# Left-side sums one group earlier, and down's first seven products one plain step earlier, in parts two and three of a macaron FFN

## The chip, the cores and the metric

The kernel runs on one core of a Trainium2 chip. The metric is the device time of one execution in microseconds; of several runs the median is taken. Before the change it is 1948.83 us (3 runs, 1947.93 to 1949.49).

## What is computed

One decoder block on a sequence of 256 tokens with 2048 channels, in float32: half an FFN, a mixer of two kinds of attention, half an FFN again, a gated embedding, a last norm. The change lies in the two FFNs:

```
D_MODEL, SEQ, D_FF = 2048, 256, 5632

def swiglu(x, w_gu, w_down):
    gate, up = jnp.split(x @ w_gu, 2, axis=-1)
    return (jax.nn.silu(gate) * up) @ w_down

h = h + 0.5 * swiglu(rms_norm(h, ffn1_norm[i]), ffn1_w_gu[i], ffn1_w_down[i])
h = h + hybrid_mixer(...)
h = h + 0.5 * swiglu(rms_norm(h, ffn2_norm[i]), ffn2_w_gu[i], ffn2_w_down[i])
gate = jax.nn.sigmoid(rms_norm(h, ple_norm[i]) @ ple_w_gate[i])
h = h + gate * (p[i] @ ple_w_proj[i])
return rms_norm(h, final_norm)
```

## The kernel before

**Split products.** Every float32 weight tile of 256 rows by 512 columns (raw, 128 x 1024 on chip) is split in two: ScalarE rounds it to its high half (whi, line 77), VectorE subtracts for the low half (wlo, line 78). The left sides are split likewise (nTh and nTl from the norm, hTh and hTl from the hidden activations). A product is then three matmuls: high times high, high times low, low times high. One such weight tile makes a *plain step*: 12 matmuls (lines 543 to 545), for two halves of 128 rows and two halves of 128 tokens.

**Seven products.** Part of each matrix product is done by a scheme with seven block products in place of eight (Strassen's, in Winograd's form). It needs sums of weight blocks and sums of left-side blocks. The weight blocks lie in four tiles R0 to R3; lines 307 and 314 add them up (on VectorE, or by an accumulating DMA on POOL's queue), line 298 (ScalarE, shi) and line 299 (VectorE, slo) split a sum; two buffers each. The left-side sums are made in `halves`: S = high + low (line 455), four subtractions and additions (line 461), and the split into Sh (ScalarE, line 463) and Sl (VectorE, line 464). `product` (lines 342 to 344) issues one of the seven, 3 matmuls for each of `ns` blocks of 128 rows (k rows of the contraction in pairs; ns is 4 for gate/up, 3 for down in parts two and three), and copies or subtracts what it has in its bank (lines 347, 350 and 352). Products 0, 4 and 6 read the left sides themselves, the others Sh and Sl.

**Parts and groups.** The hidden width is worked through in three parts of 3, 4 and 4 blocks of 512 (`PARTS`). A part has a *group* "gu" for each block (gate and up, 512 columns each, four PSUM banks), then two groups "dn" (two blocks of 512 output columns each). A gu group of parts two and three has 8 plain steps. While a group goes through its plain steps, the seven products of the *following* group are issued between them. `plan` writes this order by hand: `at[j]` is the plain step behind which the j-th product comes (in the order `SEVEN`), and `order` lists the weight splits in the same order; `next_weights` issues them some steps ahead, one sum ahead at most. `first` is the plain step of the first product: 1 between groups of one kind, 2 between kinds, 8 and 4 in two special cases. With 2, the last two products fall on one plain step, as the list is cut off at the group's last step.

**The work beside the products** runs in lanes: generators which go one step on behind each plain step (`lanes.step`). `halves` is one of them, in lane 1. `down_input` is another, in lane 0: it makes hTh and hTl of a finished gu group (line 480 on VectorE for sil, 485 for the transposition, DMAs through DRAM from ScalarE's queue and SP's, lines 502 and 503 for the split); it takes a whole group and is finished by force at the end of the next. Within this, a scheduler sets the final order of each engine's instructions; each engine works through its own in order.

The left-side sums of the first dn group of a part read the first hidden blocks of the part. Before the change `halves("dn", ...)` is added at the start of the last gu group of the part; it makes two blocks at once in its first step (1024 columns, four 256-wide steps on S), and the third in a later step (512 columns, 128-wide steps).

Of the kernel before, what the change touches and what calls it, by code (L numbers as in the profile page):

```python
# [46 lines left out]
def block_kernel(ctx, tc, a, out):  # L47
# [306 lines left out]
    def plan(n):  # L354


        def sources(name, blk):

            q, pairs = a[name + "q"][blk], a[name][blk]
            return [q[:, :, g, :].rearrange("j p n -> p j n") for g in range(q.shape[2])] + \  # L360
                [pairs[g] for g in range(pairs.shape[0])], q

        groups = []
        for p, (i0, i1) in enumerate(PARTS):
            for i in range(i0, i1):
                plain = PLAIN[n]
                if i < plain:
                    src = [([a[f"w_gu{n}0"][2 * i + b][g] for g in range(KD // 2)], None) for b in range(2)]
                else:
                    src = [sources("w_gu" + n, 2 * (i - plain) + b) for b in range(2)]  # L370
                groups.append(Group("gu", p, [x[0] for x in src], [x[1] for x in src], NS if i >= plain else 0,
                                    len(groups) % 2))
            for nb in (0, 2):
                src = [sources(f"w_down{n}{p}", nb + b) for b in range(2)]
                groups.append(Group("dn", p, [x[0] for x in src], [x[1] for x in src], NS_DOWN[p], len(groups) % 2, nb))
        if n == "2":
            src = [sources("w_behind", b) for b in range(2)]
            groups.append(Group("behind", len(PARTS), [x[0] for x in src], [x[1] for x in src], NS_BEHIND,
                                len(groups) % 2))
        if n == "1":  # L380

            groups[0].plain.sort(key=lambda x: x[1])
        made, carried = [], []
        for i, group in enumerate(groups):
            group.follower = follower = groups[i + 1] if i + 1 < len(groups) else None
            after = groups[i + 2] if i + 2 < len(groups) else None
            n_plain = len(group.plain)
            at, loads, carried = [], {0: carried}, []
            if follower is not None and follower.ns:
                first = 8 if not group.ns else 4 if follower.kind == "behind" else \  # L390
                    1 if group.kind == follower.kind else 2
                at = [min(first + j, n_plain - 1) for j in range(7)]
                if not group.ns:
                    follower.first = n

                    loads.setdefault(max(at[0] - 5, 0), []).extend(follower.loads())
                if after is not None and after.ns:
                    *three, last = after.loads(follower)
                    for x, one in zip((4, 5, 6), three):
                        loads.setdefault(at[x], []).append(one)  # L400
                    carried = [last]
            todo = []
            for j, (b, g) in enumerate(group.plain):
                todo.append(("plain", (b, g)))
                order.append(("pair", group.src[b][g]))
                if group.kind == "behind" and g == KD // 2 - 1:
                    order.append(("pair", a["w_pp"][b]))
                for x in range(7):
                    if at and at[x] == j:
                        todo.append(("seventh", x))  # L410
                        order.append(("sum", follower))
                order.extend(loads.get(j, []))
            made.append((group, todo))
        return made
# [5 lines left out]
    order += [("pair", a["w_pg"][2][g]) for g in range(KD // 2)] + [("pair", a["w_pp"][2])]  # L420
    order.append(("pair", a["w_pp"][3]))

    def halves(kind, his, los, ns, wait=0):


        for _ in range(wait):
            yield
        fp = current[0]

        sh = fp.tile([P, NS, 2, 2, P], F32R, tag="Sh", name="Sh")  # L430
        sl = fp.tile([P, NS, 2, 2, P], F32R, tag="Sl", name="Sl")

        def side(i, g):
            if i in (0, 4, 6):
                k, t = 2 * (g % 2) + (i > 0), i // 6
                c = slice(t * P, (t + 1) * P)
                return his[g // 2][:, k, c], los[g // 2][:, k, c]
            j, t = {1: (1, 1), 2: (0, 0), 3: (0, 1), 5: (1, 0)}[i]
            return sh[:, g, j, t, :], sl[:, g, j, t, :]

        sides[kind] = side

        for g0 in range(0, ns, 2):
            n = min(2, ns - g0)
            hi, lo = his[g0 // 2], los[g0 // 2]
            keep = lambda ins: ins
            if g0 and n == 1:

                keep = tc.keep_in_program_order
                yield  # L450
            if n == 2:
                x = fp.tile([P, 2 * NB], F32, tag="sil", name="S")
            else:
                x = act.tile([P, NB], F32, tag="nat", name="S", bufs=4)
            keep(nc.vector.tensor_tensor(out=x, in0=hi[:, 0:2 * n].bitcast(F32).rearrange("p k x -> p (k x)"),
                                         in1=lo[:, 0:2 * n].bitcast(F32).rearrange("p k x -> p (k x)"), op=ALU.add))
            xv = x.rearrange("p (g j t y) -> p g j t y", g=n, j=2, t=2)
            a11, a12, a21, a22 = (xv[:, :, j, t, :] for t in range(2) for j in range(2))
            for o, y, z, op in ((a22, a21, a22, ALU.subtract), (a21, a11, a21, ALU.subtract),
                                (a11, a22, a11, ALU.subtract), (a12, a11, a12, ALU.add)):  # L460
                nc.vector.tensor_tensor(out=o, in0=y, in1=z, op=op)
            sx = [y[:, g0:g0 + n].rearrange("p g j t y -> p (g j t y)") for y in (sh, sl)]
            nc.scalar.copy(sx[0], x)
            nc.vector.tensor_tensor(out=sx[1], in0=x, in1=sx[0], op=ALU.subtract)
            yield

    def ffn(n, nT, r, scale, next_norm, stat):
        xs = picker(*nT)
        late = callable(r)
        with tc.tile_pool(name="ffn", bufs=1) as fp:  # L470
# [43 lines left out]
            for group, todo in ffn_plan[n]:  # L514
# [6 lines left out]
                    lanes.add(1, halves("gu", *nT, NS))  # L521
                elif dn and group.nb and group.follower:
                    lanes.add(1, halves("behind", *nxt, NS_BEHIND, 4))
                elif not dn and group.follower.kind == "dn":
                    lanes.add(1, halves("dn", hTh[i0:], hTl[i0:], NS_DOWN[group.part]))
                if dn and group.last and nxt is None:
                    nxt = new_nT()
# [1 line left out]
                    group.new_banks()  # L529
                for kind, one in todo:  # L530
                    if kind == "seventh":
                        group.follower.product(SEVEN[one])
                        continue
                    b, g = one
                    whi, wlo = next_weights()
# [106 lines left out]
    with tc.tile_pool(name="fin", bufs=1) as fp:  # L642
# [59 lines left out]
        for t in range(2):  # L702
# [6 lines left out]
            for j in range(4):  # L709
# [5 lines left out]
                    nc.vector.tensor_scalar(out=hf[:, t, c], in0=hf[:, t, c], scalar1=rt, scalar2=None, op0=ALU.mult)  # L715
                queue = nc.sync if j % 2 else nc.scalar
                queue.dma_start(out=out[t * P:(t + 1) * P, c], in_=hf[:, t, c])


class Lanes:  # L720


    def __init__(self, n):
        self.q = [[] for _ in range(n)]
# [656 lines left out]
```

## Time and profile before

| | us |
|---|---|
| median of 3 runs | 1948.83 |
| the profiled execution | 1948.68 |
| its span in the trace | 1947.0 |
| TensorE busy in the span | 1930.5 (99%) |
| VectorE busy | 1569.3 (81%) |
| ScalarE busy | 1163.5 (60%) |

A row in order of time has the start from the span's start, the time shown, the engine (PE is TensorE, PEld its loads of the stationary operand, DVE VectorE, ACT ScalarE, POOL GpSimd, SPq the DMA-issuing queue of SP), the line, the operation, what it writes and reads, and in brackets how long the engine stood before it and what released it. In a list of waits stand the sum in us, how many, and the longest. A window has its ends and length, then the busy time and number of instructions of PE, PEld, DVE, ACT and POOL, the granted clock as a share, the DMA share and GB/s. TensorE's rows overlap, so its pace is read from one start to the next. The granted clock is full (0.999 over the span).

### The profile page before, as it was taken

The page shows a single profiled execution, that of the slowest core. Times are in us where ns is not written, and L with a number is a line of the kernel's source. Part 1 is how long each engine was busy: PE and PEld are TensorE (multiplying, and loading weights), DVE is VectorE, ACT ScalarE, POOL GpSimd, SP SyncE. Part 2 cuts the span into 40 slices and gives each one's busy share as a digit, 9 for nine tenths or more (in the row PEclk, how much of TensorE's full clock was granted, in tenths as well). Part 3 has the DMA queues.
Part 4 walks back from the last instruction along what each step waited for, and adds up shares of the span by engine and source line. Part 5 has one row for each costly group of instructions (what it writes and reads, how often), then busy time and mean ns, then how long its engine had stood idle before and what let it go on. Part 6 is the DMA issues. An engine that isn't in the chain of part 4 may idle for free.

```text
span 1947.0 us, 24130 instructions
## 1 busy us (share of the span) xinstructions
PE 1930.5 (99%) x8884; PEld 1593.0 (82%) x8884; DVE 1569.3 (81%) x1679; ACT 1163.5 (60%) x1358; POOL 148.4 (8%) x226
## 2 busy tenths in 40 slices
PE   9999999999999999999999999999999999999998
PEld 8888888888888888878788888888888888888886
DVE  7889878997889766797856579899888987888865
ACT  7656666566565557664555456566565755656654
POOL 0011100000010000010100000010000100001000
PEclk9999999999999999999999999999999999999999
DMA  8778888788887765556565786788898987888764
GB/s 314 267 238 282 254 296 273 229 294 250 279 284 240 225 219 170 176 171 208 171 204 160 242 290 227 225 291 283 243 281 249 314 260 240 272 255 293 232 213 144
DMA packets 144182, 475.04 MB, mean 244 GB/s; under 512 B 19649, under 2 KB 47297, under 8 KB 129857
## 3 DMA queue, kind: packets, MB, share of 16 engines
q1 hardware_dynamic: 107200, 302.16, 43.9%
q0 software_dynamic: 25920, 160.44, 30.2%
q10 hardware_dynamic: 10944, 10.91, 1.8%
q8 instruction: 69, 1.13, 0.2%
q14 instruction: 49, 0.39, 0.1%
HBM read 451.44 MB, written 22.02 MB: 243 GB/s over the span
## 4 chain that ended last, share of the span: by engine, by line
PE 88%; DVE 7%; DMA 3%; ACT 1%; issue 1%; POOL 0%; SPq 0%; POOLq 0%; DVEq 0%; ACTq 0%
PE d L545 5%; PE d L543 5%; PE d L544 5%; PE g L343 4%; PE g L344 4%; PE g L342 4%; PE u L544 4%; PE u L545 4%; PE u L543 4%; PE g L544 4%; PE g L545 4%; PE pj L112 4%; PE pj L113 4%; PE pj L114 4%; PE g L543 4%; PE d L343 2%
## 5 line engine op out<-in xcount | busy, mean ns | idle before, releaser
L77 ACT CAST whi<-raw 128x1024 fp32r<-128x1024 f32 (+1 forms) x489 | 512.1, 1050 | 422.7 <-PE pj L114 99.0
L78 DVE TENSOR_TENSOR wlo<-raw,whi 128x1024 fp32r<-128x1024 f32 (+1 forms) x489 | 592.3, 1218 | 162.3 <-ACT whi L77 161.2
L299 DVE TENSOR_TENSOR slo<-R,shi 128x2048 fp32r<-128x2048 f32 (+2 forms) x224 | 444.9, 1989 | 140.0 <-ACT shi L298 138.2
L298 ACT CAST shi<-R 128x2048 fp32r<-128x2048 f32 (+2 forms) x224 | 373.5, 1671 | 128.5 <-DVE R L307 62.7
L112 PE MATMUL pj<-whi,nTh 128*128 128x512 f32 x448 | 179.4, 401 | 0.0
L113 PE MATMUL pj<-wlo,nTh 128*128 128x512 f32 x448 | 175.2, 391 | 1.1 <-DVE wlo L78 1.1
L114 PE MATMUL pj<-whi,nTl 128*128 128x512 f32 x448 | 174.9, 390 | 0.0
L543 PE MATMUL d<-whi,hTh 128*128 128x512 f32 x448 | 174.5, 390 | 0.0
L544 PE MATMUL d<-wlo,hTh 128*128 128x512 f32 x448 | 174.3, 389 | 0.0
L545 PE MATMUL d<-whi,hTl 128*128 128x512 f32 x448 | 173.4, 389 | 0.0
L544 PE MATMUL g<-wlo,nTh 128*128 128x512 f32 x400 | 156.0, 390 | 0.5 <-DVE wlo L78 0.5
L544 PE MATMUL u<-wlo,nTh 128*128 128x512 f32 x400 | 155.7, 389 | 0.4 <-DVE wlo L78 0.4
L545 PE MATMUL g<-whi,nTl 128*128 128x512 f32 x400 | 155.8, 389 | 0.0
L545 PE MATMUL u<-whi,nTl 128*128 128x512 f32 x400 | 155.7, 389 | 0.0
L543 PE MATMUL g<-whi,nTh 128*128 128x512 f32 x400 | 155.3, 390 | 0.0
L543 PE MATMUL u<-whi,nTh 128*128 128x512 f32 x400 | 154.1, 389 | 0.0
L307 DVE TENSOR_TENSOR R<-R 128x2048 f32<-128x2048 f32 (+2 forms) x68 | 135.8, 1996 | 0.1
L113 PEld LDWEIGHTS pj<-wlo,nTh 128*128 128x128 f32 x448 | 84.2, 188 | 18.9 <-DVE wlo L78 2.6
L543 PEld LDWEIGHTS d<-whi,hTh 128*128 128x128 f32 x448 | 84.1, 188 | 18.2 <-ACT hTh L502 1.0
L545 PEld LDWEIGHTS d<-whi,hTl 128*128 128x128 f32 x448 | 84.1, 188 | 17.8
L114 PEld LDWEIGHTS pj<-whi,nTl 128*128 128x128 f32 x448 | 84.1, 188 | 17.5
L544 PEld LDWEIGHTS d<-wlo,hTh 128*128 128x128 f32 x448 | 84.1, 188 | 17.4
(332 smaller groups left out, 3444.1 us busy)
## 6 DMA issues: line engine op xcount, KB each, us to landing
raw<-in_w_gu SPq DMA_DIRECT2D x199, 512.0 KB, 5.7
raw<-in_w_down SPq DMA_DIRECT2D x112, 512.0 KB, 6.9
raw<-in_w_in SPq DMA_DIRECT2D x112, 512.0 KB, 3.4
R<-in_w_gu2q POOLq DMA_DIRECT2D x54, 1024.0 KB, 8.6
R<-in_w_gu1q POOLq DMA_DIRECT2D x48, 1024.0 KB, 8.6
raw<-in_w_out SPq DMA_DIRECT2D x32, 512.0 KB, 4.5
tT<-scr SPq DMA_DIRECT2D x22, 512.0 KB, 5.0
R<-in_w_down11q POOLq DMA_DIRECT2D x12, 768.0 KB, 6.2
```

The lines of the kernel that those rows point to most:

```text
L77: nc.scalar.copy(hi[:, j, :], raw[:, j, :])
L78: nc.vector.tensor_tensor(out=lo[:, j, :], in0=raw[:, j, :], in1=hi[:, j, :], op=ALU.subtract)
L112: nc.tensor.matmul(outs[t], xh[:, c], whi[:, j, :], start=st, stop=False)
L113: nc.tensor.matmul(outs[t], xh[:, c], wlo[:, j, :], start=False, stop=False)
L114: nc.tensor.matmul(outs[t], xl[:, c], whi[:, j, :], start=False, stop=sp)
L298: keep(nc.scalar.copy(hi, w))
L299: nc.vector.tensor_tensor(out=lo, in0=w, in1=hi, op=ALU.subtract)
L307: keep(nc.vector.tensor_tensor(out=self.raw[x], in0=self.raw[x], in1=self.raw[y], op=ALU.add))
L343: nc.tensor.matmul(out, xh, wlo[:, g, :], start=False, stop=False, skip_group_check=True)
L543: nc.tensor.matmul(out, xh[:, c], whi[:, j, :], start=st, stop=False, skip_group_check=True)
L544: nc.tensor.matmul(out, xh[:, c], wlo[:, j, :], start=False, stop=False, skip_group_check=True)
L545: nc.tensor.matmul(out, xl[:, c], whi[:, j, :], start=False, stop=sp, skip_group_check=True)
```

## The change

Three things, in the last gu group but one, the last gu group and the first dn group of parts two and three of both FFNs:

1. `first` is 1 in place of 2 where a gu group of these parts has a dn group as follower: the seven products come behind plain steps 1 to 7, one each, in place of 2 to 6 and two at 7.
2. `halves("dn", ...)` is added earlier: in the gu group before the last, behind the product at place 5 (the last that reads Sh). As it runs before the second block's hTh is finished, it picks the blocks when it needs them (`Later`).
3. With `at_once=1` it makes one block of 128 rows at a time (512 columns) in place of two; the first two blocks still go in one step of the lane.

Part one keeps the old way. No matmul, weight load or DMA is added or left out.

```diff
             if follower is not None and follower.ns:
                 first = 8 if not group.ns else 4 if follower.kind == "behind" else \
-                    1 if group.kind == follower.kind else 2
+                    1 if group.kind == follower.kind or group.part and follower.kind == "dn" else 2
                 at = [min(first + j, n_plain - 1) for j in range(7)]
...
-    def halves(kind, his, los, ns, wait=0):
+    def halves(kind, his, los, ns, wait=0, at_once=2):
...
-        for g0 in range(0, ns, 2):
-            n = min(2, ns - g0)
-            hi, lo = his[g0 // 2], los[g0 // 2]
+        for g0 in range(0, ns, at_once):
+            n = min(at_once, ns - g0)
+            k0 = 2 * (g0 % 2)
+            hi, lo = (x[g0 // 2][:, k0:k0 + 2 * n] for x in (his, los))
             keep = lambda ins: ins
-            if g0 and n == 1:
+            if g0 == 2 and n == 1:
...
-            yield
+            if not g0 % 2 + n == 1 or g0 + n == ns:
+                yield
...
-                elif not dn and group.follower.kind == "dn":
+                elif not dn and group.follower.kind == "dn" and not group.part:
                     lanes.add(1, halves("dn", hTh[i0:], hTl[i0:], NS_DOWN[group.part]))
...
                     if kind == "seventh":
-                        group.follower.product(SEVEN[one])
+                        follower = group.follower
+                        follower.product(SEVEN[one])
+                        if group.part and not dn and one == 5 and follower.kind == "gu" and \
+                                follower.follower.kind == "dn":
+                            p = PARTS[group.part][0]
+                            lanes.add(1, halves("dn", Later(hTh, p), Later(hTl, p), NS_DOWN[group.part], 0, 1))
                         continue
...
+class Later:
+
+
+    def __init__(self, blocks, first):
+        self.blocks, self.first = blocks, first
+
+    def __getitem__(self, i):
+        return self.blocks[self.first + i]
```

**What it makes of the order.** The first place is TensorE, from the last matmul of the second product of the first dn group (its bank is d0) to the first matmul that reads the fourth product's low weights (slo, L343); u0 and u1 are up's banks in the last gu group of part two. Before:

```order
L344 MATMUL d0_2790<-shi_2740,Sl_2725 128x512
L344 MATMUL d1_2789<-shi_2802,Sl_2725 128x512
L544 MATMUL u1_2454<-wlo_2844,nTh_102 128x512
...
L543 MATMUL u0_2453<-whi_2879,nTh_102 128x512
L342 MATMUL d0_2788<-shi_2838,hTh_2085 128x512
L544 MATMUL u0_2453<-wlo_2880,nTh_102 128x512
...
L545 MATMUL u1_2454<-whi_2879,nTl_106 128x512
L343 MATMUL d0_2788<-slo_2839,hTh_2085 128x512
```

And in the changed kernel:

```order
L344 MATMUL d0_2780<-shi_2727,Sl_2684 128x512
L343 MATMUL d1_2779<-slo_2793,Sh_2683 128x512
L344 MATMUL d1_2779<-shi_2792,Sl_2684 128x512
...
L551 MATMUL u1_2454<-wlo_2870,nTh_102 128x512
L342 MATMUL d0_2778<-shi_2825,hTh_2085 128x512
L552 MATMUL u1_2454<-whi_2869,nTl_106 128x512
...
L552 MATMUL u1_2454<-whi_2869,nTl_106 128x512
L343 MATMUL d0_2778<-slo_2826,hTh_2085 128x512
```

The last row is 17 matmuls behind the first before, and 22 in the changed kernel. From the fifth product's last matmul to the seventh's first read of slo it is 17 and 22 as well.

The second place is VectorE from the first 1536-wide slo on (the first down product's weights), in the last gu group but one of part two and the start of the last. Before:

```order
L299 TENSOR_TENSOR slo_2692<-R_2548,shi_2691 128x1536
L480 SCALAR_TENSOR_TENSOR sil_2526<-u0_2152,rstd2_515,sil_2526 128x512
L480 SCALAR_TENSOR_TENSOR sil_2526<-u1_2153,rstd2_515,sil_2526 128x512
L503 TENSOR_TENSOR hTl_2383<-tT_2604,hTh_2382 128x4x4x32 x2
L78 TENSOR_TENSOR wlo_2687<-raw_2685,whi_2686 128x1024
L307 TENSOR_TENSOR R_2548<-R_2548,R_2584 128x1536
L485 STREAM_TRANSPOSE tb_2721<-sil_2526 128x4x128 x2
L78 TENSOR_TENSOR wlo_2736<-raw_2734,whi_2735 128x1024
L455 TENSOR_TENSOR S_2726<-hTh_2085,hTl_2086 128x1024
L299 TENSOR_TENSOR slo_2741<-R_2548,shi_2740 128x1536
```

And in the changed kernel:

```order
L299 TENSOR_TENSOR slo_2666<-R_2548,shi_2665 128x1536
L462 TENSOR_TENSOR S_2685<-S_2685 128x128
L307 TENSOR_TENSOR R_2548<-R_2548,R_2584 128x1536
L462 TENSOR_TENSOR S_2685<-S_2685 128x128
L456 TENSOR_TENSOR S_2693<-hTh_2085,hTl_2086 128x512
L462 TENSOR_TENSOR S_2685<-S_2685 128x128
L462 TENSOR_TENSOR S_2693<-S_2693 128x128
L462 TENSOR_TENSOR S_2685<-S_2685 128x128
L462 TENSOR_TENSOR S_2693<-S_2693 128x128
L482 SCALAR_TENSOR_TENSOR sil_2526<-u0_2152,rstd2_515,sil_2526 128x512
L462 TENSOR_TENSOR S_2693<-S_2693 128x128
L465 TENSOR_TENSOR Sl_2684<-S_2685,Sh_2683 128x512
```

The two blocks' sums (S_2685 and S_2693, taking turns) now stand in front of sil, hTl, the transposition and the splits that come with them. Behind these twelve come another small step on S_2693, the second sil, a wlo, the second Sl, two hTl, a slo, a transposition, a sum R, a transposition, and then the wlo of the last gu group's fourth plain step, whose first reader stands 55 matmuls behind the first matmul of that group.

The third place is ScalarE at the same point. Before, the first two blocks' cast Sh stands in front of the copy of the first product's bank:

```order
L298 CAST shi_2740<-R_2548 128x1536
L491 DMA scr2_2757<-tb_2721 32x4x256 x4
L77 CAST whi_2763<-raw_2762 128x1024
L463 CAST Sh_2724<-S_2726 128x1024
L347 COPY d0_2788<-d1_2789 128x512
L298 CAST shi_2802<-R_2548 128x1536
```

And in the changed kernel in two halves right behind the second down cast shi:

```order
L77 CAST whi_2710<-raw_2709 128x1024
L298 CAST shi_2727<-R_2548 128x1536
L464 CAST Sh_2683<-S_2685 128x512
L77 CAST whi_2748<-raw_2747 128x1024
L464 CAST Sh_2683<-S_2693 128x512
L504 CAST hTh_2382<-tT_2604 128x4x4x32 x2
L77 CAST whi_2798<-raw_2797 128x1024
L347 COPY d0_2778<-d1_2779 128x512
```

Sh has moved ahead of two weight casts, and waits for S on VectorE in a queue in which those casts stand behind it.

More of the change, by code (lines that the diff above doesn't have):

```diff
@@ L454, in halves @@
                 x = act.tile([P, NB], F32, tag="nat", name="S", bufs=4)
-            keep(nc.vector.tensor_tensor(out=x, in0=hi[:, 0:2 * n].bitcast(F32).rearrange("p k x -> p (k x)"),
-                                         in1=lo[:, 0:2 * n].bitcast(F32).rearrange("p k x -> p (k x)"), op=ALU.add))
+            keep(nc.vector.tensor_tensor(out=x, in0=hi.bitcast(F32).rearrange("p k x -> p (k x)"),
+                                         in1=lo.bitcast(F32).rearrange("p k x -> p (k x)"), op=ALU.add))
             xv = x.rearrange("p (g j t y) -> p g j t y", g=n, j=2, t=2)
```

## The prediction

> **What bounds the kernel now.** I read the page first, then the list of waits by engine, then the windows around the places that the diff touches, and last the rows there in order of time. The page says that TensorE is the bound and that little is left.
>
> ```profile
> PE 1930.5 (99%) x8884; PEld 1593.0 (82%) x8884; DVE 1569.3 (81%) x1679; ACT 1163.5 (60%) x1358; POOL 148.4 (8%) x226
> ```
>
> Only time in which TensorE stands can be won. The waits of its weight loads name what belongs to this change: a down product (d) that waits for the low half of its summed weights (slo, line 299), and one that waits for its left-side sum (Sh, line 463).
>
> ```profile
> PEld d L343 <- DVE slo L299: 4.8, 8, 0.6
> PEld d L342 <- ACT Sh L463: 1.1, 4, 0.3
> ```
>
> Eight and four are two and one at each of four places: the transition from gate/up to down in parts two and three, in both FFNs. The windows show the first and the last of the four doing the same to a hundredth (TensorE 41.64 of 42 us, VectorE 37.2), so one is worked out and taken four times.
>
> ```profile
> 340.00:382.00 42.00, 41.64 (x182) 33.46 (x181) 37.24 (x42) 24.75 (x26) 3.96 (x6) 1.00 0.77 238
> 1733.00:1775.00 42.00, 41.64 (x181) 33.46 (x180) 37.23 (x40) 24.75 (x26) 3.91 (x6) 1.00 0.77 238
> ```
>
> Busy time hides a stall, since a late matmul is only shown longer (0.50 for 0.39). So I go by starts.
>
> ```profile
> 340.08 0.39 PE L543 MATMUL g<-whi,nTh 128*128 128x512 f32 x1
> ...
> 350.28 0.39 PE L543 MATMUL g<-whi,nTh 128*128 128x512 f32 x1
> ...
> 362.74 0.39 PE L544 MATMUL u<-wlo,nTh 128*128 128x512 f32 x1
> ...
> 368.20 0.40 PE L545 MATMUL u<-whi,nTl 128*128 128x512 f32 x1
> 368.73 0.50 PE L343 MATMUL d<-slo,hTh 128*128 128x512 f32 x1
> 369.07 0.40 PE L344 MATMUL d<-shi,hTl 128*128 128x512 f32 x1
> ...
> 376.57 0.39 PE L342 MATMUL d<-shi,hTh 128*128 128x512 f32 x1
> 377.18 0.50 PE L343 MATMUL d<-slo,hTh 128*128 128x512 f32 x1 [0.22 <-DVE slo L299]
> ...
> 379.12 0.39 PE L543 MATMUL d<-whi,hTh 128*128 128x512 f32 x1
> ```
>
> From 350.28 to 362.74 stand 55 matmuls in the program: 12.46 / 55 = 0.2265 us each. From 362.74 to 379.12 stand 67, which would take 15.18 and took 16.38: 1.20 us are lost. The two waits for slo make 0.80 of it: 0.53 - 0.23 = 0.30 at 368.73, 0.61 - 0.23 = 0.38 at 377.18, and each time 0.11 more, because the matmul behind a late weight load comes 0.34 after it (368.73 to 369.07). The rest is the wait for Sh and slightly long steps around the three. Four places: **4.8 us, the ceiling of what this change can win.**
>
> **The change part by part. The stalls that go.** Both waits for slo are one chain. Row by row:
>
> ```profile
> 364.49 0.39 PE L344 MATMUL d<-shi,Sl 128*128 128x512 f32 x1
> 364.92 0.57 ACT L347 COPY d<-d 128x512 f32<-128x512 f32 x1 [1.99 <-PE d L344]
> 365.40 1.48 ACT L298 CAST shi<-R 128x1536 fp32r<-128x1536 f32 x1
> 366.92 1.76 DVE L299 TENSOR_TENSOR slo<-R,shi 128x1536 fp32r<-128x1536 f32 x1 [2.65 <-ACT shi L298]
> ...
> 372.94 0.39 PE L344 MATMUL d<-shi,Sl 128*128 128x512 f32 x1
> 373.37 0.59 ACT L350 COPY part<-d 128x512 f32<-128x512 f32 x1
> 373.85 1.48 ACT L298 CAST shi<-R 128x1536 fp32r<-128x1536 f32 x1
> 375.37 1.76 DVE L299 TENSOR_TENSOR slo<-R,shi 128x1536 fp32r<-128x1536 f32 x1 [0.35 <-ACT shi L298]
> ```
>
> A product's last matmul releases ScalarE's copy of its bank 0.43 later; the cast of the product after next stands behind that copy (0.48), VectorE's slo behind the cast (1.52), and TensorE takes it 1.81 after: 4.24 us both times (364.49 to 368.73, 372.94 to 377.18). The order puts 17 matmuls between, 17 x 0.2265 = 3.85, so 0.39 is missing. In the changed order 22 matmuls stand between at both places (the last product no longer shares the last plain step): 22 x 0.2265 = 4.98, 0.74 to spare. Both stalls go.
>
> The wait for Sh goes too: the sum below, carried on, has the third block's Sh ready 1.3 us before the matmul that reads it.
>
> **What comes instead.** VectorE gets the left-side sums of two blocks in the preceding group and the first steps of the last one, and it does not idle from the first 1536-wide slo on. The durations, from rows of before (a step is the distance to the next start, since ends overlap):
>
> ```profile
> 336.36 1.76 DVE L299 TENSOR_TENSOR slo<-R,shi 128x1536 fp32r<-128x1536 f32 x1 [1.10 <-ACT shi L298]
> 338.03 1.41 DVE L480 SCALAR_TENSOR_TENSOR sil<-u,rstd,sil 128x512 f32<-128x512 f32 x2
> 339.35 1.29 DVE L503 TENSOR_TENSOR hTl<-tT,hTh 128x512 fp32r<-128x512 f32 x2
> 340.55 1.22 DVE L78 TENSOR_TENSOR wlo<-raw,whi 128x1024 fp32r<-128x1024 f32 x1
> 341.69 1.75 DVE L307 TENSOR_TENSOR R<-R 128x1536 f32<-128x1536 f32 x1
> 343.35 1.30 DVE L485 STREAM_TRANSPOSE tb<-sil 128x512 f32<-128x512 f32 x2
> 344.57 1.18 DVE L78 TENSOR_TENSOR wlo<-raw,whi 128x1024 fp32r<-128x1024 f32 x1
> ...
> 348.48 0.42 DVE L461 TENSOR_TENSOR S<-S 128x256 f32<-128x256 f32 x1
> 348.81 1.75 DVE L307 TENSOR_TENSOR R<-R 128x1536 f32<-128x1536 f32 x1
> 350.48 1.34 DVE L461 TENSOR_TENSOR S<-S 128x256 f32<-128x256 f32 x3
> 351.74 1.22 DVE L78 TENSOR_TENSOR wlo<-raw,whi 128x1024 fp32r<-128x1024 f32 x1
> ...
> 356.52 0.28 DVE L461 TENSOR_TENSOR S<-S 128x128 f32<-128x128 f32 x1
> 356.72 1.22 DVE L78 TENSOR_TENSOR wlo<-raw,whi 128x1024 fp32r<-128x1024 f32 x1
> ```
>
> The critical one is the low half (wlo) for the fourth plain step of the last gate/up group. Before it the changed order has, from that slo on: 2 slo x 1.67, 2 sums R x 1.66, 8 small steps S x 0.20 (356.52 to 356.72), one 512-wide sum, 2 Sl and 2 hTl x 0.60 (339.35 to 340.55 for two; a 512-wide step each), 2 sil x 0.66, one wlo 1.14, 2 transposes x 0.61, and the wlo itself with its whole 1.22: 3.34 + 3.32 + 1.60 + 3.00 + 1.32 + 1.14 + 1.22 + 1.22 = 16.16. So it lands at 336.36 + 16.16 = 352.52, and the matmul can go 0.05 later (366.92 + 1.76 = 368.68 for 368.73). TensorE wants it 55 matmuls behind 340.08: 352.54, and the load of its weights one matmul ahead. The matmul behind then goes at 352.57 + 0.34 = 352.91 where 352.77 is due: 0.14 lost. With the slightly long steps that go with stalls (1.20 where the named ones give 1.01) I take 0.17 a place. The bounds: nothing if VectorE is 0.15 quicker than this sum, 0.3 if it is 0.15 slower, for rounding to 0.01 over some 20 steps.
>
> What follows is not late. The third block's sum (0.60) and a slo come next on VectorE: 352.43 + 0.60 + 1.76 = 354.79, for the matmul 10 behind 352.91, at 355.18. Then a small step and a wlo: 354.70 + 0.20 + 1.22 = 356.12, for one 5 further, at 356.31. Then, start to start, a small step, a wlo, two dependent small steps, and Sh on ScalarE: 356.04 + 0.20 + 1.14 + 0.33 + 0.29 = 358.00, Sh (0.62) at 358.7, for the matmul 16 behind 356.31, at 359.9. From there the room grows.
>
> Costed at nothing: 6 more VectorE instructions a place are in the 16.16 as far as they stand before that matmul; halving adds only 2 x 0.60 - 1.13 = 0.07 to the first sum, 0.06 to Sl, and nothing to the subtractions (8 x 0.20 against 0.33 + 1.26). ScalarE's halved Sh cast hides in an engine busy 24.75 of 42. No DMA is added. On SP one load of the transposed hidden block (tT) falls behind two weight loads; its reader (hTl) stood 24 us behind it:
>
> ```profile
> 353.47 0.33 SPq L496 DMA_DIRECT2D tT<-scr  x1
> ...
> 377.70 1.28 DVE L503 TENSOR_TENSOR hTl<-tT,hTh 128x512 fp32r<-128x512 f32 x2
> ```
> POOL's order is unchanged, and its loads are released by the same slo as before, about one plain step (12 x 0.2265 = 2.7 us) earlier along with their readers.
>
> [...]
>
> **Sum.** 1.20 - 0.17 = 1.03 a place, 4.1 us in all. The profiled execution took 1948.68 (span 1947.0), 0.15 under the median 1948.83; from the median: **1944.7 us.** A measurement of this kernel can tell about 0.2% from no change: 3.9 us, 1944.93. The forecast lies 0.2 beyond it, so whether it is called faster or the same is nearly open.
>
> **The rivals.** *The small steps are dearer.* The 0.20 is from single S steps that wait for nothing just before them. When each waits for the one before, as the three at 350.48 do (1.26 / 3 = 0.42 for 0.42 long), a 128-wide one takes 0.28 + 0.05 = 0.33. Eight of them: 8 x 0.13 = 1.04 more on a full VectorE, all of it in front of the critical wlo: 1.21 lost for 1.20 won, 1948.8. For it: the queue has no gap. Against: the order lets two halves take turns, so a step mostly waits for the one before last. Part of it would give 1945 to 1948. [...]
>
> *Slower: VectorE stands before Sl.* The first Sl needs ScalarE's cast Sh, which stands behind the second down cast shi; that one waits for the buffer that TensorE's matmul ahead of 340.08 leaves. By the same rows the matmul before 340.08 leaves it 0.43 after its start, at 340.28, Sh starts at 341.68 and ends at 342.30, and Sl is due 5.99 behind 336.36, at 342.35: no room. If ScalarE waits for S here as it did elsewhere, VectorE stands as long, and all of it reaches the critical wlo.
>
> ```profile
> ACT Sh L463 <- DVE S L461: 30.1, 12, 5.3
> ```
>
> That wait was 30.1 / 12 = 2.5 us in the mean. Price: 2.5 + 0.17 lost against 1.20 won, 4 x 1.47 = 5.9: 1954.7. It makes the kernel slower by over 0.2% from a standing of 2.0 us on. Against: the S steps that Sh needs end at 341.58 by the same sum, before ScalarE is free.
>
> *It does not do what it says:* the chain of 4.24 grows by as much as the distance (a copy that finds ScalarE busy for 0.85), and the waits for slo stay: 1948.8.
>
> **How the numbers follow.** Forecast 0.66, dearer small steps 0.22, slower 0.07, stalls that stay 0.05. In the forecast the new loss runs from 0 to 0.3: 1944.0 to 1945.2, and the bound is crossed below 0.22, three quarters of it: faster 0.50. Same: 0.16 + 0.22 + 0.05 = 0.43. Slower 0.07. The range goes from 1944.0 less 0.4 for the spread of runs (1947.93 to 1949.49) to two thirds of the way to the first rival's end, 1947.4; the last two rivals and the rest of the first are left out, under 0.2. The likeliest alone: 1943.6 to 1945.6.
>
> **What would show it.** Right: the waits "d L343 for slo" and "d L342 for Sh" gone from the weight loads' list; one short wait of a gate matmul (line 551) for wlo at each place; the 67 matmuls' stretch at 15.2 to 15.4. Wrong in size: a wait at line 551 above 0.3, with S steps 0.33 apart on VectorE. Wrong: VectorE idle before Sl for 2 us, or waits for slo still at eight.

## The result, and the profile after

| | before | changed |
|---|---|---|
| median of 15 runs each, us | 1948.83 (1947.35 to 1949.68) | 1944.74 (1944.07 to 1945.96) |
| changed / before, 95% interval | | 0.998 (0.9972 to 0.9988) |
| profiled execution, us | 1948.68, span 1947.0 | 1945.28, span 1943.6 |

The kernel is faster by 4.09 us, 0.21%: just beyond the 0.2% that the prediction took as the bound of what can be told, and its interval, 0.12 to 0.28% faster, reaches to both sides of that bound, but not to zero. Of all executions behind this document one took far longer, 6208.34 us, in the second series of the order of products alone; the median of that series is the same without it.

The changed kernel's page has 24 more instructions on VectorE and 4 on ScalarE, and as many matmuls on TensorE:

```profile
PE 1928.1 (99%) x8884; PEld 1594.0 (82%) x8884; DVE 1570.4 (81%) x1703; ACT 1164.1 (60%) x1362; POOL 148.4 (8%) x226
```

In the list of waits of its weight loads the down products' rows "d L343 for slo" (4.8 us) and "d L342 for Sh" (1.1 us) are gone. A row of a gate matmul that waits for wlo has come (us in total, times, longest); four of its seven are the four places, with 0.3 each:

```profile
PEld g L551 <- DVE wlo L78: 2.7, 7, 0.8
```

The windows around the first and the last place in the changed kernel. The first lies where that of before lay, the last 3 us earlier, since the work there has moved.

```profile
340.00:382.00 42.00, 42.00 (x186) 34.52 (x186) 38.49 (x47) 26.80 (x30) 4.84 (x7) 1.00 0.80 242
1730.00:1772.00 42.00, 42.00 (x186) 34.53 (x185) 38.45 (x47) 27.33 (x30) 4.79 (x7) 1.00 0.80 239
```

TensorE has 42.00 of 42 where it had 41.64, and four or five matmuls more in the same stretch (186 for 182 and 181): one microsecond's worth. VectorE is busier, 38.5 for 37.2. But busy time still hides what is lost, so here too the starts decide. TensorE at the first place of the changed kernel, in order of time:

```profile
340.96 0.39 PE L550 MATMUL g<-whi,nTh 128*128 128x512 f32 x1
...
353.45 0.50 PE L551 MATMUL g<-wlo,nTh 128*128 128x512 f32 x1
353.79 0.39 PE L552 MATMUL g<-whi,nTl 128*128 128x512 f32 x1
...
375.36 0.39 PE L343 MATMUL d<-slo,hTh 128*128 128x512 f32 x1
...
386.47 0.39 PE L552 MATMUL d<-whi,hTl 128*128 128x512 f32 x1
```

The first row is the first matmul of the last gate/up group, the last one stands 200 matmuls behind it. Those 200 take 200 x 0.2265 = 45.30 at TensorE's pace; here they took 45.51, so 0.21 is lost. Before, the same 200 ran from 340.08 to 386.60, and 1.23 was lost (from the starts in ns). **This difference is the measure in what follows: the loss at a place, worked out in the same way from each kernel's rows.**

| us lost at the place | 1st | 2nd | 3rd | 4th | median of the runs |
|---|---|---|---|---|---|
| before | 1.23 | 1.26 | 1.23 | 1.23 | 1948.83 |
| changed | 0.21 | 0.25 | 0.23 | 0.25 | 1944.74 |

The four differences sum to 4.0. Set against each other matmul by matmul (both kernels have the same 8884), the two executions differ by more than 0.1 us in two other stretches. One is those first 12 us, where the changed kernel's execution falls 0.88 behind. The other is near 1829, where ScalarE of before stood 2.17 for a weight that was still being fetched, and TensorE lost 0.53. Nothing that the change touches is in either. With them the two profiled executions lie 3.40 apart, and not 4.0.

### The profile page after: what moved, and what is told of

The parts are those of the page before. It is cut to its first block, busy times and chain, and to the rows that moved or that the text cites. A ratio compares the mean times of both kernels' runs of the same rounds, so it can differ in the third digit from the quotient of the medians.

```text
span 1943.6 us, 24163 instructions
## 1 busy us (share of the span) xinstructions
PE 1928.1 (99%) x8884; PEld 1594.0 (82%) x8884; DVE 1570.4 (81%) x1703; ACT 1164.1 (60%) x1362; POOL 148.4 (8%) x226
## 4 chain that ended last, share of the span: by engine, by line
PE 92%; DVE 5%; DMA 2%; issue 1%; ACT 0%; POOL 0%; SPq 0%; POOLq 0%; DVEq 0%; ACTq 0%
PE d L550 5%; PE d L552 5%; PE d L551 5%; PE u L551 5%; PE u L552 5%; PE u L550 5%; PE g L343 5%; PE g L342 5%; PE g L344 5%; PE g L551 4%; PE g L552 4%; PE pj L112 4%; PE pj L113 4%; PE pj L114 4%; PE g L550 4%; PE d L344 3%
```

## The experiments

The theory on record: the gain comes from the order of products and plain steps, which puts 22 matmuls instead of 17 over a chain of 4.24 us (copy, cast, slo); the sums that begin earlier make it possible and cost 0.17 a place. The main rival says that what is won goes to VectorE's full queue. What neither says is which of the two halves of the change does what, so each is run alone first. The medians are of 4 (early sums alone) to 11 executions. The measured losses of all kernels stand here together; the sections below read them.

| us lost at the place | 1st | 2nd | 3rd | 4th | median | ratio to before, 95% interval |
|---|---|---|---|---|---|---|
| order of products alone | 0.17 | 0.15 | 0.15 | 0.14 | 1944.28 | 0.9978 (0.9969 to 0.9987) |
| the same again | 0.16 | 0.17 | 0.15 | 0.17 | 1944.46 | 0.9976 (0.9967 to 0.9985) |
| the whole change again | 0.23 | 0.21 | 0.26 | 0.22 | 1944.71 | 0.9978 (0.9969 to 0.9987) |
| early sums alone | 3.31 | 2.60 | 5.77 | 2.07 | 1957.7 | 1.0045 (1.0028 to 1.0062) |
| early sums alone, tT's load later | 2.07 | 2.05 | 3.07 | 2.17 | 1954.06 | 1.0028 (1.0017 to 1.004) |
| change, one block a lane step | 0.43 | 0.41 | 0.44 | 0.48 | 1945.27 | 0.9983 (0.9974 to 0.9992) |
| change, VectorE op added | 0.78 | 0.76 | 0.78 | 0.77 | 1946.83 | 0.9992 (0.9982 to 1.0001) |
| before, ScalarE copy added | 2.21 | 2.25 | 2.21 | 2.25 | 1951.83 | 1.0016 (1.0006 to 1.0027) |
| change, ScalarE copy added | 0.24 | 0.25 | 0.23 | 0.24 | 1944.76 | 0.998 (0.9969 to 0.999) |
| order of products, part one too | 0.15 | 0.17 | 0.16 | 0.14 | 1947.89 | 0.9995 (0.9985 to 1.0005) |

### The order of products alone

From before, only the one line of the order; the left-side sums stay where they were, two blocks at once.

```
-                    1 if group.kind == follower.kind else 2
+                    1 if group.kind == follower.kind or group.part and follower.kind == "dn" else 2
```

> Only the table entry of the change: the seven products of the first down group come one plain step earlier; the left-side sums start where they did before, two blocks at once. Distance theory (the stalls were a chain of 4.24 us with 17 matmuls between; the earlier products alone make room): the eight waits of down matmuls for slo are gone, each place loses 0.0 to 0.3 us instead of 1.20, the time is 3.6 to 4.8 us under before, like the whole change or a few tenths better, since VectorE is spared the sums in front of the critical wlo. Rival (the early sums carry the gain): the second product finds Sh and Sl not made, a new wait for Sh or Sl of 0.5 us or more at each place, and the time is at most 2 us under before.

Measured: 1944.28 us, 0.15 lost a place. That is the whole gain, and 0.07 to 0.09 a place more than the change has. So **the order alone does it**, and the early sums are not what makes it possible. In this kernel's waits of the weight loads the down products' rows for slo and Sh are gone, and a short wait for the low half of the sum has come in their place:

```profile
PEld d L344 <- DVE Sl L464: 0.8, 4, 0.2
```

Why the late sums don't hurt is seen on its three engines in order of time. First ScalarE and VectorE:

```profile
354.77 1.05 ACT L463 CAST Sh<-S 128x1024 fp32r<-128x1024 f32 x1 [5.42 <-DVE S L461]
...
360.66 0.59 ACT L347 COPY d<-d 128x512 f32<-128x512 f32 x1
...
369.09 0.59 ACT L350 COPY part<-d 128x512 f32<-128x512 f32 x1 [0.78 <-PE d L344]
369.57 1.49 ACT L298 CAST shi<-R 128x1536 fp32r<-128x1536 f32 x1
```
```profile
355.86 1.23 DVE L464 TENSOR_TENSOR Sl<-S,Sh 128x1024 fp32r<-128x1024 f32 x1 [0.59 <-ACT Sh L463]
...
371.18 1.75 DVE L299 TENSOR_TENSOR slo<-R,shi 128x1536 fp32r<-128x1536 f32 x1
```

And TensorE, the first reader of Sl, and then the two ends of the chain:

```profile
357.20 0.44 PE L344 MATMUL d<-shi,Sl 128*128 128x512 f32 x1
...
368.66 0.39 PE L344 MATMUL d<-shi,Sl 128*128 128x512 f32 x1
...
375.46 0.39 PE L343 MATMUL d<-slo,hTh 128*128 128x512 f32 x1
```

The low half of the sum is done at 355.86 + 1.23 = 357.09 and read at 357.20. The weight load waited 0.2 for it; TensorE itself loses 0.05, on the matmul behind. The products that need the sum are placed behind it, since the scheduler that writes the order moves the second and third product to where their operands are: the second begins 69 matmuls behind the group's first, where it began 59 behind before and 45 in the changed kernel. ScalarE stands 5.42 us for the sum, but TensorE loses nothing by what is queued behind. The first of the two chains has 22 matmuls between its ends, and as its copy, at 360.66, has to wait for the weight cast ahead of it, 0.3 to spare. The second has much room: copy at 369.09, 0.43 behind the product's last matmul, cast, slo done at 372.93, and its reader at 375.46, 30 matmuls behind (368.66 + 30 x 0.2265 = 375.46), so some 2.5 to spare.

### The early sums alone

The changed kernel with that one line put back:

```
-                    1 if group.kind == follower.kind or group.part and follower.kind == "dn" else 2
+                    1 if group.kind == follower.kind else 2
```

> The other half of the change: early left-side sums, one block at a time, with the products where they were before (the last two on one plain step). Distance theory: the chain of copy, cast and slo is as short of matmuls as before somewhere among the last products, 0.8 to 1.2 us lost at each place, and the time is 0 to 1.6 us under before. Rival (early sums carry the gain): 0.3 us or less lost a place, and 3.6 us or more under before.

Measured: 1957.7 us, slower than before by 0.45%, with 2.07 to 5.77 lost a place. The expectation that the chain stays as short of matmuls as before was wrong. Counted in TensorE's rows, 25 matmuls stand between the ends of the first chain and 23 between those of the second, for 17 and 17 before, although the last two products still share a plain step: by this count either half of the change takes away the stalls of before. The loss comes from elsewhere. VectorE and ScalarE of this kernel in order of time show a form of the prediction's slower rival, at the third block's sum:

```profile
354.94 1.27 DVE L462 TENSOR_TENSOR S<-S 128x128 f32<-128x128 f32 x4
```
```profile
356.24 0.62 ACT L464 CAST Sh<-S 128x512 fp32r<-128x512 f32 x1 [4.48 <-DVE S L462]
356.77 1.48 ACT L298 CAST shi<-R 128x1536 fp32r<-128x1536 f32 x1
358.15 1.04 ACT L77 CAST whi<-raw 128x1024 fp32r<-128x1024 f32 x1
...
372.38 1.05 ACT L77 CAST whi<-raw 128x1024 fp32r<-128x1024 f32 x1 [4.05 <-DMA raw<-in_w_down]
```

ScalarE stands 4.48 us before the cast Sh until VectorE has the sum, and behind Sh in its queue are a cast shi and a cast whi. TensorE comes for that whi before it is there (0.37 late at 359.24, and the matmuls of slo behind it): 1.05 lost at each of the four places. The last row is a second loss that the prediction did not have: ScalarE stands 4.05 for a down weight that is still being fetched, and the copy that heads the second chain is queued behind it. It comes at 374.37, 3.47 behind the product's last matmul instead of 0.43, and the seventh product is late for that. At the first place the cause is on SP, whose waits from 350 to 375 us are:

```profile
SPq L74 <- DVE wlo L78: 18.3, 6, 4.9
SPq L498 <- DMA scr<-tb: 8.1, 1, 8.1
```

SP stood 8.1 us before the load of tT, for the store that tT reads back. It issued that load at 361.21, and the down weights queued behind it only from 361.63 on. In all this kernel's ScalarE waited 16.5 us for down weights, before 7.8, the changed kernel 2.1.

### The early sums alone, with tT's load later

The same kernel, with the load of tT two lane steps later, so that two down loads stand ahead of it, as in the changed kernel, instead of one:

```
-                for _ in range(2 if last else 4):
+                for _ in range(2 if last else 6):
...
-                for _ in range(last or 6):
+                for _ in range(last or 4):
```

> The early sums alone, with the load of the transposed hidden block (tT) asked for two lane steps later, so that it stands behind one more weight load on SP's queue. In the early sums alone SP stood 8.1 us on that load, waiting for the transposed block's writes, and ScalarE then stood 4 to 5 us for a weight load queued behind it. If that queue is what made it 9 us slower than before, the 4 to 5 us wait of ScalarE for raw shrinks to under 2 us and the time falls to 1946 to 1950; the chain of copy, cast and slo with 17 matmuls between it stays, 0.8 to 1.2 us lost a place. Rival (early sums cost it, by VectorE's load): the wait for raw may go, but the time stays over 1953.

Measured: 1954.06 us, 3.6 less, but above the 1946 to 1950 that was expected if the queue were the cause. ScalarE's wait for down weights fell from 16.5 to 5.4 us. What stayed in this kernel is the stand for the sum, and waits for slo, three a place:

```profile
355.39 0.62 ACT L464 CAST Sh<-S 128x512 fp32r<-128x512 f32 x1 [4.48 <-DVE S L462]
```
```profile
PEld d L343 <- DVE slo L299: 9.4, 12, 1.6
```

These are not the waits of the chain over 17 matmuls; here too 25 and 23 stand between its ends. The first follows the stand of 4.48, with the late whi, and costs 1.05 a place, as without the edit. The second is the seventh product's slo. TensorE, from the fifth product's last matmul to the slo that is 23 matmuls behind it, and ScalarE between them:

```profile
370.05 0.39 PE L344 MATMUL d<-shi,Sl 128*128 128x512 f32 x1
...
376.07 0.50 PE L343 MATMUL d<-slo,hTh 128*128 128x512 f32 x1 [0.65 <-DVE slo L299]
```
```profile
371.22 1.14 ACT L504 CAST hTh<-tT 128x512 fp32r<-128x512 f32 x2 [1.71 <-DMA tT<-scr]
372.27 0.58 ACT L350 COPY part<-d 128x512 f32<-128x512 f32 x1
```

The copy comes 2.22 behind the matmul that releases it, not 0.43, because ScalarE stands 1.71 for tT, the very load that this edit asks for later, and then casts it. That costs 0.9 to 1.0 a place, and 1.9 at the third. (The third wait, some 75 matmuls on, lies behind the stretch of the table; it costs 0.7 at the first and third place.) So the order of the loads on SP is worth at least 3.6 of the 8.9 us by which the early sums alone are slower; the edit took only a part of it, as it put a stand for tT where one for a down weight had been. How much of the 3.6 is the stretch at half the clock that the last section shows, some 1.6 us of the profiled execution of the kernel without this edit, was not tried.

### One block a lane step

The changed kernel, without the lines that let two blocks' subtractions take turns within one lane step:

```
-            if not g0 % 2 + n == 1 or g0 + n == ns:
-                yield
+            yield
```

> The changed kernel, but its lane goes on one step after every block, so the second block's sum comes one plain step later. If the new wait for wlo in the last gate/up group is only VectorE's load in front of it, it shrinks from about 0.19 to 0.0 to 0.1 us; but what is taken off there stands later in the queue, and the distance theory, which needs only the chain, leaves no room for a slo that VectorE makes later: 0.1 to 0.4 lost a place at another wait. Time: within 1 us of the changed kernel. Rival (the wait for wlo is a late weight cast and not VectorE's queue): the wait for wlo stays at 0.19.

Measured: 1945.27 us, 0.44 lost a place. The waits of its weight loads from 340 to 390 us:

```profile
PEld d L343 <- DVE slo L299: 0.3, 1, 0.3
PEld g L550 <- DVE wlo L78: 0.2, 1, 0.2
PEld d L342 <- ACT shi L298: 0.2, 1, 0.2
```

The wait for wlo is shorter, and one for slo has come 11 us later. It is the chain again. From the second product's last matmul to the fourth product's first slo:

```profile
359.23 0.39 PE L344 MATMUL d<-shi,Sl 128*128 128x512 f32 x1
...
363.46 0.50 PE L343 MATMUL d<-slo,hTh 128*128 128x512 f32 x1
```

These are 4.23 us, the chain's length, and the order of this kernel has 18 matmuls between the two, 18 x 0.2265 = 4.08: 0.15 missing, although its products start as early as in the changed kernel. In all the same sums cost 0.2 a place more when each block has its lane steps for itself.

### One operation more on VectorE

The changed kernel with one 512-wide addition more, between the first two blocks' sums, on the full queue in front of the critical wlo:

```
+            if at_once == 1 and g0 == 1:
+                junk = act.tile([P, NB], F32, tag="junk", name="dose", bufs=1)
+                nc.vector.tensor_tensor(out=junk, in0=x, in1=x, op=ALU.add)
```

> The changed kernel with one more 512-wide VectorE operation (0.60 us from start to start) behind the second block's sum, whose result nobody reads. If VectorE's queue has no gap between the first down slo and the critical wlo, TensorE loses 0.4 to 0.65 us more at each place, 1.6 to 2.6 us in all. Rival (the queue has room, the wait for wlo comes from ScalarE or a transfer): under 0.15 more a place, and the time stays within 0.6 us of the changed kernel.

Measured: 1946.83 us, 0.77 lost a place, 0.54 more than without. The two ends of VectorE's stretch, the first 1536-wide slo and the critical wlo:

```profile
337.67 1.76 DVE L299 TENSOR_TENSOR slo<-R,shi 128x1536 fp32r<-128x1536 f32 x1 [0.50 <-ACT shi L298]
...
353.25 1.18 DVE L78 TENSOR_TENSOR wlo<-raw,whi 128x1024 fp32r<-128x1024 f32 x1
```

From the start of the one to the end of the other are 353.25 + 1.18 - 337.67 = 16.76 us, 0.59 more than the 16.17 of the changed kernel (worked out below), for 0.60 added: VectorE has no room here, and nearly all of it reaches TensorE. But the stand itself is at another matmul. This kernel's waits of the weight loads from 340 to 380 us:

```profile
PEld d L342 <- ACT shi L298: 0.7, 1, 0.7
PEld u L554 <- DVE wlo L78: 0.3, 1, 0.3
```

The longest wait is now for shi, ScalarE's cast. That cast is no later than in the changed kernel, 11.40 us behind the group's first matmul in both (352.79 - 341.39, 352.36 - 340.96). But the order, which the scheduler made anew for this kernel, has a matmul that reads it 55 behind the group's first, in front of the reader of wlo; in the changed kernel the first such reader stands 65 behind. So an added operation can also change the order, and where TensorE stands shows only which operand the order asks for first.

### One copy more on ScalarE, in before and in the change

Into both kernels one 512-wide copy (0.48 start to start) behind the copies of the second and the fourth product, at the four places: right inside the chain of 4.24 us.

```
+            def dose(src):
...
+                junk = act.tile([P, NB], F32, tag="junk", name="dose", bufs=1)
+                tc.keep_in_program_order(nc.scalar.copy(junk, src))
```

Expected of before with it:

> The kernel before with one more 512-wide ScalarE copy (0.48 us), read by nobody, behind the two copies of a bank that head the two chains. Distance theory: 4.24 becomes 4.72 with 17 matmuls between, each of the two waits for slo grows by 0.48, 0.9 to 1.0 us more lost a place, 3.6 to 4.0 us in all. Rival (slo waits for VectorE or a transfer and not for this chain): no wait grows by more than 0.15.

Expected of the changed kernel with it:

> The changed kernel with the same ScalarE copies. Distance theory: 4.72 is under the 4.98 of 22 matmuls, and there is no new wait for slo; places lose what they lose in the changed kernel (about 0.2) and the time is within 0.8 us of it. Rival (the stalls went because ScalarE or VectorE became freer, with no room left): 0.4 us more a place.

Measured: before with it 1951.83 us, 3.1 more, the changed kernel with it 1944.76, the same as without. Before, with the copy, ScalarE and then TensorE in order of time:

```profile
365.11 0.57 ACT L353 COPY d<-d 128x512 f32<-128x512 f32 x1 [1.99 <-PE d L344]
365.59 0.59 ACT L350 COPY dose<-d 128x512 f32<-128x512 f32 x1
366.07 1.49 ACT L298 CAST shi<-R 128x1536 fp32r<-128x1536 f32 x1
```
```profile
368.41 0.40 PE L555 MATMUL u<-whi,nTl 128*128 128x512 f32 x1
369.40 0.50 PE L343 MATMUL d<-slo,hTh 128*128 128x512 f32 x1 [0.59 <-DVE slo L299]
```

The cast shi is 0.96 behind the copy's start instead of 0.48, and the matmul of slo comes 0.99 after the one ahead of it, where it came 0.53 after: of 0.48 added, 0.46 arrives. At the second wait 0.49 arrives (0.38 late before, 0.87 now). The loss goes from 1.23 to 2.21 a place, by 0.98. In the changed kernel the waits of the weight loads with a gate matmul show nothing new, and no down product waits for slo:

```profile
PEld g L561 <- DVE wlo L78: 2.8, 7, 0.6
```

So in before the chain has no room at all, and in the change more than 0.48. That is what 17 and 22 matmuls say (0.39 missing, 0.74 to spare). For the first chain of the change it is a clean test, with 22 matmuls still between its ends, and its room falls from 0.76 to 0.27; for the second the scheduler has put 26 between them. The four places of before sum to 4.0 more; the median shows 3.1.

### The order of products in part one too

The order alone, with the exception for part one taken out:

```
-                    1 if group.kind == follower.kind else 2
+                    1 if group.kind == follower.kind or follower.kind == "dn" else 2
```

> The table entry alone, in all three parts: the first down group of part one, whose products are shorter (2 blocks) and whose sums wait for hidden blocks finished later, also starts one plain step earlier. Distance theory: part one had no wait for slo to lose, so nothing is won there; its left-side sums are asked for one step earlier and VectorE is as full there, so 0 to 1.5 us are lost at each of the two places of part one: 1944 to 1947.5. Rival (an earlier start always helps): under 1943.8.

Measured: 1947.89 us, 3.6 above the order alone, though parts two and three lose the same 0.15. The waits of its weight loads have a row that the others lack:

```profile
PEld d L342 <- ACT shi L298: 2.9, 4, 0.8
```

In part one two places lose 1.29 and 1.35 us more than before over 200 matmuls (waits of 0.43 and 0.72 with what follows them, at 162 and 163 us in the first): there the cast comes too late for products that stand earlier. This accounts for 2.6 of the 3.6.

### The two versions again

To see whether the order alone is better than the whole change, both once more, on the same chip.

> The table entry alone, timed again beside the whole change. If the early sums only cost (0.05 to 0.1 us a place on VectorE in the last gate/up group, and a short wait for Sh in the following one that the entry alone did not show), it is 0.3 to 0.7 us faster than the whole change, too little for these runs to separate for certain. Rival (the early sums bring something that the profile of one run did not show): it is slower than the whole change.

> The whole change, timed again in the same call: 1944.2 to 1945.2, and 0.3 to 0.7 us over the table entry alone if the early sums only cost.

Measured: 1944.46 and 1944.71 us. The losses at the places repeat, 0.16 and 0.23 in the mean, which makes 0.3 us for the kernel; the medians differ by 0.25, and by 0.46 in the first series of each. The two intervals of the ratio (0.9967 to 0.9985, 0.9969 to 0.9987) lie on one another. By the rows the order alone is the better version by 0.3 us; the times do not show it.

## Why the prediction was right, and where its reasons were not

**The ceiling, 1.20 a place.** Right: 1.23 to 1.26 over the 200 matmuls. The 0.80 given for the two waits for slo is a slip: 0.30 + 0.38 + 2 x 0.11 are 0.90, and with 0.11 for the wait for Sh that is the 1.01 used further on.

**The stalls that go.** Right, to a hundredth. The chain in the changed kernel, ScalarE and then VectorE, at the seventh product's slo:

```profile
370.80 0.59 ACT L350 COPY part<-d 128x512 f32<-128x512 f32 x1 [0.78 <-PE d L344]
371.28 1.48 ACT L298 CAST shi<-R 128x1536 fp32r<-128x1536 f32 x1
```
```profile
372.80 1.76 DVE L299 TENSOR_TENSOR slo<-R,shi 128x1536 fp32r<-128x1536 f32 x1 [0.27 <-ACT shi L298]
```

Copy to cast 0.48, cast to slo 1.52, slo usable 1.81 after: at 374.61. TensorE takes it at 375.36: 0.75 to spare where 0.74 was predicted. The rival in which the chain grows with the distance did not occur, and the ScalarE copy showed from outside that the room is there.

The reason given for the 22, that the last product no longer shares the last plain step, is not borne out. In the early sums alone it does share it, and 25 and 23 matmuls stand between; with one block a lane step it does not, and at the first chain there are 18. The number comes out of the order that the scheduler made, and the prediction had it right because it was counted there.

**What comes instead.** VectorE of the changed kernel, from the first 1536-wide slo to the critical wlo:

```profile
337.23 1.76 DVE L299 TENSOR_TENSOR slo<-R,shi 128x1536 fp32r<-128x1536 f32 x1 [0.50 <-ACT shi L298]
...
341.58 0.90 DVE L462 TENSOR_TENSOR S<-S 128x128 f32<-128x128 f32 x4
342.39 0.75 DVE L482 SCALAR_TENSOR_TENSOR sil<-u,rstd,sil 128x512 f32<-128x512 f32 x1
...
343.25 0.69 DVE L465 TENSOR_TENSOR Sl<-S,Sh 128x512 fp32r<-128x512 f32 x1
...
352.21 1.19 DVE L78 TENSOR_TENSOR wlo<-raw,whi 128x1024 fp32r<-128x1024 f32 x1
```

No row after the first, those left out included, has idle time before it, so the sum of the steps is the time: 352.21 + 1.19 - 337.23 = 16.17, predicted 16.16. The matmul came 0.05 behind, at 353.45, where the pace wants it at 340.96 + 55 x 0.2265 = 353.42, and the one behind it 0.34 after: the 0.14 of the prediction. The whole loss is 0.21 to 0.25, predicted 0.17; slightly long steps around the wait make the rest (the ten from 353.79 to 356.10 take 0.231 each instead of 0.2265).

**The dearer small steps** did not occur in the changed kernel. The four that take turns at 341.58 go to the next start in 342.39 - 341.58 = 0.81, 0.20 each, not 0.33. The size of the rival was right where the steps do not take turns: the third block's four in the early sums alone, each waiting for the one before, go 0.33 apart ((1.27 - 0.29) / 3, from the row at 354.94 there). In the changed kernel the cost of halving, an estimate of 0.07 + 0.06 = 0.13 a place from the rows of before, stands: the sum of VectorE's steps, the halved ones included, was 16.17 for 16.16.

**VectorE standing before Sl** did not occur in the changed kernel, though as near as predicted. ScalarE's row there:

```profile
342.59 0.61 ACT L464 CAST Sh<-S 128x512 fp32r<-128x512 f32 x1
```

It ends at 343.20, Sl starts at 343.25. In the early sums alone ScalarE did stand for S, 4.48 us long, but for the third block's sum and not the first; VectorE stood only 0.69 for that Sh, and what came late were the casts behind it. With the loads on SP's queue this made that kernel 8.9 us slower.

**The sum**, 1.03 a place and 4.1 in all, was 1.0 and 4.0, and 4.09 in the medians. That 1944.7 met the median of 1944.74 so closely is luck: the 15 executions spread over 1.9 us, and two misses of the same sign cancel, the ceiling (1.24 in the mean for 1.20) and the new loss (0.24 for 0.17).

**What the prediction had wrong** is who earns it. It wrote that the wait for Sh goes because the sums are early, and counted their cost, 0.17 a place, as the price of the order. The order alone runs as fast, with the sums late and the wait for Sh gone all the same, because the scheduler moves the products that need them. Nor do the early sums need the order for the distance of the chains, which is 25 and 23 without it. With it their stand is harmless: in the changed kernel ScalarE stands 5.08 us for the third block's sum, and TensorE loses nothing there. The early sums fill VectorE's queue to the point where 0.21 to 0.25 is lost, against 0.15 without them. Comparing only the two whole kernels, it took the two halves of the change to need each other.

**tT's load on SP**, costed at nothing, was no cost in the change: SP does not stand for it at all from 340 to 380 us, where before stood 7.2. The step holds, though not with the 24 us that were shown for it. VectorE's hTl is not the first reader; ScalarE's cast hTh is, at 369.59 before, 16 us behind the load, and at 376.27 in the change, 17 behind, where the load took 8.5 to land. In the early sums alone that cast stands in front of the copy that heads the second chain, and moving the load behind one more weight load won 3.6 us.

## What to carry to other kernels

Where a bound engine waits for a chain through other engines, count its own instructions between the two ends in the order that was built (the plan does not give the number: 25 and 23 stood there with the last two products on one step), multiply by its pace, and set that against the chain's row-to-row length: here 17, 18 and 22 against 4.24 us told which version stands and by how much, and a known piece of work put into the chain shows from outside which of the two is longer. When a change has two halves, run each alone: one of these was the whole gain, and the other by itself a loss of 8.9 us. The place of a load in its queue is a change of its own: in the early sums alone SP stood 8.1 us for one load, the down weights behind it came later, and moving that load behind one more of them was worth 3.6 us.

## What the runs showed of the hardware that was not expected

In the profiled execution of the early sums alone TensorE stood twice in a row at the third place, 1.58 and 1.79 us from start to start, with one matmul between 1524.22 and 1527.59, and then ran for 3 us at a granted clock of one half. The windows of that kernel, the stands, what followed, and the return:

```profile
1524.00:1527.60 3.60, 1.12 (x5) 0.38 (x3) 2.63 (x4) 3.60 (x4) 0.00 (x0) 1.00 1.01 418
1528.30:1531.30 3.00, 3.00 (x8) 2.32 (x7) 3.00 (x4) 0.00 (x0) 0.06 (x1) 0.50 0.83 272
1531.30:1535.00 3.70, 3.70 (x17) 3.04 (x16) 3.70 (x5) 0.93 (x1) 0.12 (x1) 0.99 0.35 96
```

The granted clock is 0.50 in the second, with 8 matmuls in 3.00 us where 17 stand in 3.70 after it. At 0.43 from start to start instead of 0.2265, 8 matmuls cost some 1.6 us more, which is part of the 5.77 lost at that place. At the first place this kernel has two stands in a row as well, 0.71 and 1.79 us, and its granted clock is 1.00 over the window from 340 to 382 us. What makes the clock fall after the one pair and not after the other was not shown by these runs.
